# A streaming encoder step: keys of the running streams turned by VectorE's block transpose

## The chip, the cores and the metric

The kernel runs on one core of a Trainium2 chip. The metric is the device time of one execution in microseconds (us), as the median of several runs. TensorE (PE in the profile, with PEld for its weight loads) multiplies, VectorE (DVE), ScalarE (ACT) and GpSimd (POOL) work element by element, and SyncE (SP) issues every DMA of this kernel. Each engine runs its own queue of instructions in order and waits on semaphores for the others.

## The reference, cut to what matters

One inference step of a one-layer trunk. 1,024 rows of a new prompt and 8 running streams of 16 rows each, 1,152 rows of 1,024 columns, pass three token mixers (stick-breaking attention, Mamba-2, forgetting attention), then a cross-attention over 256 memory rows with 4 heads of 256 channels, and a SwiGLU. The running streams bring their own keys and values: 1,024 cached rows for each attention and 256 memory rows per stream. The change touches the places where their keys meet the queries:

```python
def sb_attend(q, k, v, q_pos, k_pos):            # k: past 1,024 rows and 16 new ones
    z = jnp.einsum('bqhd,bkhd->bhqk', q, k).astype(jnp.float32) * (HEAD_DIM ** -0.5)
    ...
def cross_attend(u, mk, mv, wq, wo):             # mk: cache_mem_k, (8, 256, 4, 256) for the streams
    q = jnp.einsum('bnd,de->bne', u, wq).reshape(b, n, X_HEADS, X_HEAD_DIM)
    s = jnp.einsum('bnhd,bmhd->bhnm', q, mk.astype(q.dtype)).astype(jnp.float32) * (X_HEAD_DIM ** -0.5)
    pr = jax.nn.softmax(s, axis=-1)
    o = jnp.einsum('bnhm,bmhd->bnhd', pr, mv.astype(jnp.float32)).astype(u.dtype)
    return jnp.einsum('bne,ed->bnd', o.reshape(b, n, D_MODEL), wo)
```

Both products sum over channels, so TensorE needs the keys with channels on the partitions, while memory holds them row by row.

## The kernel before, in words

Large products are made in three matmuls (`mm3`, lines 328 to 330): each factor is split into a rounded part `hi` (ACT, line 292) and a remainder `lo` (POOL in pieces of 256 columns, line 132), and hi x hi, hi x lo and lo x hi are summed in PSUM. Weights come in units of 1,024 columns (`w_unit`, line 307): two raw buffers of 528 columns, of which the ring has four (`wr`), are loaded (line 317) and split into a pair `wh`, `wl`, of which the ring has three each.

Stages in order of time: norm and memory projection; the stick-breaking attention with the input projection woven into it (about 140 to 430 us); the forgetting attention with Mamba-2 (to about 700); the output projection (`finish_rows`); the cross-attention (about 800 to 985), where each head's query projection (`x_query`) is woven with the attention of the head before (`x_prompt` for the prompt, `x_sample` for the streams); its output projection; the SwiGLU. The order of instructions on each engine is written by a scheduler that simulates the program with priorities, when the kernel is built; a change in one place can move instructions elsewhere.

The stick-breaking streams (`decode_units`, m = 0) work on two streams p at a time and half of the past (512 rows) at a time. `load_k` (lines 876 to 892) loads 512 rows of one stream in two DMAs into two raw buffers (line 882), PE turns eight blocks of 128x128 into two PSUM banks (line 888), and ACT copies them into `kf` (line 890), a buffer of the `wh` or `wl` ring. Four matmuls in four column groups (`quads`, line 873) then give 512 scores each. This happens 16 times; m = 1, the forgetting attention, has 16 more of the same code.

In `x_sample` two streams' memory rows of one head are loaded by two DMAs (line 1558), PE turns them in 8 transposes of 128x128 (line 1578), ACT copies one bank and DVE the other (line 1580) into `kf`, and `products` (line 1564) multiplies them with `zq`, the streams' queries placed so that each group of 32 PSUM rows gets two streams. There are 4 such loads a head. The channels of a head are split in two halves of 128, db, both for queries and keys.

## Time and profile before

| | us |
|---|---|
| Three runs, median (lowest to highest) | 1884.5 (1882.29 to 1886.88) |
| The profiled execution | 1882.33 |
| its span in the profile | 1880.6 |
| PE busy | 1826.0 |
| DVE busy | 886.7 |
| ACT busy | 802.5 |
| POOL busy | 618.4 |

In the profile's rows an instruction is named by its line in the kernel before, its engine and operation, and the tiles that it writes and reads ("pst<-ident,wr": into pst from ident and wr). A group's row gives the count, the time in which at least one of them ran, the mean of one in ns, and behind the next bar the engine's idle time just ahead of them and what ended it. A tile's row gives the shortest, middle and longest duration in ns and the first and last start. A row of the timeline gives start and duration. PE's matmuls overlap: one of 0.34 us may be followed by the next after 0.18.

### The profile page before, as it was taken

The page shows a single profiled execution, that of the slowest core. Times are in us where ns is not written, and L with a number is a line of the kernel's source. Part 1 is how long each engine was busy: PE and PEld are TensorE (multiplying, and loading weights), DVE is VectorE, ACT ScalarE, POOL GpSimd, SP SyncE. Part 2 cuts the span into 40 slices and gives each one's busy share as a digit, 9 for nine tenths or more (in the row PEclk, how much of TensorE's full clock was granted, in tenths as well). Part 3 has the DMA queues.
Part 4 walks back from the last instruction along what each step waited for, and adds up shares of the span by engine and source line. Part 5 has one row for each costly group of instructions (what it writes and reads, how often), then busy time and mean ns, then how long its engine had stood idle before and what let it go on. Part 6 is the DMA issues. An engine that isn't in the chain of part 4 may idle for free.

```text
span 1880.6 us, 32355 instructions
## 1 busy us (share of the span) xinstructions
PE 1826.0 (97%) x12136; PEld 1632.1 (87%) x12136; DVE 886.7 (47%) x1798; ACT 802.5 (43%) x1719; POOL 618.4 (33%) x921
## 2 busy tenths in 40 slices
PE   7999998999999999999999989999999999999998
PEld 5899877888967768899988889999999999888886
DVE  3412323475657862444443596333333334455554
ACT  6533543545456861344432464333333333344443
POOL 7622424445116663101112107445444542000000
PEclk9999999999999999999999999999999999999999
DMA  9465654437588882245585124333222223657572
GB/s 333 153 188 152 210 144 130 144 109 205 175 262 266 281 288 91 108 134 177 173 284 191 68 73 119 90 85 76 71 71 71 71 71 93 217 184 246 171 247 86
DMA packets 291036, 296.64 MB, mean 158 GB/s; under 512 B 80060, under 2 KB 242852, under 8 KB 290880
## 3 DMA queue, kind: packets, MB, share of 16 engines
q1 hardware_dynamic: 290880, 294.57, 49.9%
q8 instruction: 96, 1.57, 0.3%
q14 instruction: 60, 0.49, 0.1%
HBM read 225.12 MB, written 69.91 MB: 157 GB/s over the span
## 4 chain that ended last, share of the span: by engine, by line
PE 83%; DMA 5%; DVE 4%; POOL 3%; ACT 2%; issue 2%; SPq 0%; DVEq 0%; POOLq 0%; ACTq 0%
PE psd L1869 11%; PE psd L328 10%; PE psd L329 10%; PE psd L330 10%; PE pst L1869 8%; PE pss L1869 4%; PE pss L328 4%; PE pss L329 4%; PE pss L330 4%; PE pso L1869 2%; PE pst L328 2%; PE pst L329 2%; PE pst L330 2%; PE pso L593 1%; DMA act<-acsc 1%
## 5 line engine op out<-in xcount | busy, mean ns | idle before, releaser
L132 POOL TENSOR_TENSOR wl<-wr,wh 128x256 fp32r<-128x256 f32 (+2 forms) x184 | 142.3, 807 | 229.5 <-ACT wh L292 208.6
L328 PE MATMUL psd<-act,wh 128*128 128x384 f32 x528 | 182.3, 346 | 0.0
L330 PE MATMUL psd<-act,wl 128*128 128x384 f32 x528 | 181.2, 343 | 0.6 <-POOL wl L132 0.6
L329 PE MATMUL psd<-act,wh 128*128 128x384 f32 x528 | 181.7, 344 | 0.0
L1869 PE MATMUL pst<-bT,tr 128*128 128x256 f32 (+1 forms) x1068 | 155.0, 293 | 0.0
L1869 PEld LDWEIGHTS pst<-bT,tr 128*128 128x128 f32 x1068 | 144.9, 188 | 0.1
L330 PE MATMUL psd<-wh,act 128*128 128x512 f32 (+3 forms) x424 | 136.7, 323 | 0.0
L329 PE MATMUL psd<-wl,act 128*128 128x256 f32 (+3 forms) x414 | 134.0, 324 | 1.9 <-POOL wl L132 1.9
L328 PE MATMUL psd<-wh,act 128*128 128x256 f32 (+3 forms) x414 | 132.9, 325 | 0.7 <-DMA act<-osc 0.5
L1869 PE MATMUL psd<-bT,tr 128*128 128x320 f32 (+1 forms) x912 | 132.8, 295 | 0.6 <-POOL tr L132 0.6
L1869 PEld LDWEIGHTS psd<-bT,tr 128*128 128x128 f32 x912 | 124.7, 188 | 1.0 <-POOL tr L132 0.9
L132 POOL TENSOR_TENSOR tr<-u,tr 128x256 fp32r<-128x256 f32 x110 | 82.8, 781 | 101.7 <-ACT tr L1705 83.8
L253 POOL TENSOR_SCALAR sm<-sm 128x1 f32<-128x1 f32 (+2 forms) x27 | 9.1, 337 | 298.4 <-ACT y L1980 209.0
L1844 DVE TENSOR_TENSOR tr<-tr,pst 128x256 f32<-128x256 f32 (+1 forms) x86 | 38.6, 449 | 139.9 <-ACT tr L1841 106.6
L330 PEld LDWEIGHTS psd<-act,wl 128*128 128x128 f32 x528 | 99.2, 188 | 3.2 <-issue 1.9
L132 POOL TENSOR_TENSOR ws<-ws 128x256 f32<-128x256 f32 (+2 forms) x100 | 69.2, 719 | 98.7 <-DVE ws L522 90.4
L328 PEld LDWEIGHTS psd<-act,wh 128*128 128x128 f32 x528 | 99.4, 188 | 2.5 <-issue 1.8
L329 PEld LDWEIGHTS psd<-act,wh 128*128 128x128 f32 x528 | 99.3, 188 | 1.9 <-issue 1.5
L132 POOL TENSOR_TENSOR tr<-raw,tr 128x256 fp32r<-128x256 f32 x94 | 69.2, 764 | 83.8 <-ACT tr L1705 75.7
L1705 ACT CAST tr<-u 128x512 fp32r<-128x512 f32 x130 | 76.8, 620 | 28.6 <-PE pst L1869 5.6
L292 ACT CAST wh<-wr 128x512 fp32r<-128x512 f32 (+2 forms) x90 | 52.4, 621 | 82.9 <-PE psd L330 32.1
L329 PEld LDWEIGHTS psd<-wl,act 128*128 128x128 f32 x414 | 78.9, 191 | 10.0 <-POOL wl L132 3.6
(645 smaller groups left out, 4674.4 us busy)
## 6 DMA issues: line engine op xcount, KB each, us to landing
u<-w_down SPq DMA_DIRECT2D x40, 512.0 KB
raw<-w_down SPq DMA_DIRECT2D x26, 512.0 KB
st<-qksc SPq DMA_DIRECT2D x48, 256.0 KB
wr<-w_in SPq DMA_DIRECT2D x44, 256.0 KB
tr<-hidsc SPq DMA_DIRECT2D x55, 192.0 KB
hidsc<-tr SPq DMA_DIRECT2D x34, 288.0 KB
qksc<-sg SPq DMA_DIRECT2D x48, 192.0 KB
wr<-cache_sb_k SPq DMA_DIRECT2D x32, 256.0 KB
```

Of the source, the lines that this page charges most:

```text
L132: POOL.tensor_tensor(out=out[:, a0:a1], in0=in0[:, a0:a1], in1=in1[:, a0:a1], op=op)
L253: POOL.tensor_scalar(v, ss, inv, EPS, ALU.mult, ALU.add)
L292: ACT.copy(hi, raw)
L328: PE.matmul(out, ah, bh, start=start, stop=False)
L329: PE.matmul(out, ah, bl, start=False, stop=False)
L330: PE.matmul(out, al, bh, start=False, stop=stop)
L593: return PE.matmul(po[r:r + 64, q_], vt[:, 2 * (k0 + i) + j, :], pfs[i][:, sl], start=start and k0 == 0 and (j == 0 or qp > 0), stop=k0 + ...
L1705: ACT.copy(hi, src)
L1844: DVE.tensor_tensor(out=at(out, g), in0=at(x, g), in1=ps[g][:, :GW[g]], op=op)
L1869: PE.matmul(dst[g][:, :GW[g]], x[:, ka], y[:, k, :], start=start and k == 0 and m == 0, stop=stop and k == 3 and m == 2, skip_group_check= ...
```

## The change

**Memory keys of the streams.** Each load takes two streams' 512 rows of one head. Four DMAs bring it, one for each 64 channels into 32 partitions, 16 rows a partition in runs of 64 channels. DVE transposes blocks of 32x32 in place (`DVE.transpose`, STREAM_TRANSPOSE in the order). Then partition 32 g + j holds channels 64 g + 2 j and 64 g + 2 j + 1, so that the two halves of the channels are now the even and the odd ones. The keys are read by `products` in steps of two elements, and their rows come in another order (t, i), which the exponential of `x_softmax` puts back (`blocks`). The transposes on PE, the copies by ACT and DVE and the `kf` buffers go. Stream pairs are neighbours now (b0 + b for b0 + 2 b), which the placement of queries and the last transpose make good.

**Query weights.** The even and odd channels need `wq` split that way: `x_query` makes two units of 256 columns by four row blocks, both needed by each half db, with a split that sorts columns by parity (`split_parted`: ACT and POOL read in steps of two; as many instructions as before). The prompt's memory keys are turned on PE from every second column (`mkn[:, mb, db::2]`).

**Cached stick-breaking keys.** `load_k` for m = 0 loads one stream's 512 rows in four DMAs into one raw buffer, runs of 32 channels (128 bytes), and DVE transposes 128x1024 from it into `kf`, writing in steps of 16 elements. Eight transposes on PE and two copies by ACT go. m = 1 stays as it was.

**Raw buffers.** The ring has two of 1,056 columns where it had four of 528; `w_unit` and `load_k` use the two halves of one.

The core of the diff:

```diff
--- before.py
+++ after.py
@@ -302,12 +302,23 @@
 
     def raw_t():
 
-        return ring.tile([P, 528], F32, tag="wr", name="wr", bufs=4)
-
-    def w_unit(srcs, k0, nk, raw=None, pair=None, eng=POOL):
+        return ring.tile([P, 1056], F32, tag="wr", name="wr", bufs=2)
+
+    def split_parted(hi, lo, raw):
+        h, l = (t.rearrange("p (k x m) -> p k x m", x=2, m=P) for t in (hi, lo))
+        r = raw.rearrange("p (k m x) -> p k x m", x=2, m=P)
+        ACT.copy(h, r)
+        for k in range(h.shape[1]):
+            POOL.tensor_tensor(out=l[:, k], in0=r[:, k], in1=f32(h[:, k]), op=ALU.subtract)
+
+    def w_unit(srcs, k0, nk, raw=None, pair=None, eng=POOL, parted=False):
 
         n = sum(s[2] for s in srcs)
-        raws = [raw_t(), raw_t()] if raw is None else [raw]
+        if raw is None:
+            raw = raw_t()
+            raws = [raw[:, :528], raw[:, 528:]]
+        else:
+            raws = [raw]
         nk_ = nk // len(raws)
         for i, r in enumerate(raws):
             rv = r[:, :nk_ * n].rearrange("p (k n) -> p k n", n=n)
@@ -320,7 +331,10 @@
         hi, lo = pair or unit_pair()
         for i, r in enumerate(raws):
             sl = slice(i * nk_ * n, (i + 1) * nk_ * n)
-            split_into(hi[:, sl], lo[:, sl], r[:, :nk_ * n], eng)
+            if parted:
+                split_parted(hi[:, sl], lo[:, sl], r[:, :nk_ * n])
+            else:
+                split_into(hi[:, sl], lo[:, sl], r[:, :nk_ * n], eng)
         return (hi[:, :nk * n].rearrange("p (k n) -> p k n", n=n),
                 lo[:, :nk * n].rearrange("p (k n) -> p k n", n=n))
 
@@ -874,9 +888,17 @@
                                                 moving(g // 2, g % 2), start=True, stop=True) for g in (3, 0, 1, 2)])
 
             def load_k(hf, b2):
-                rvs = []
+                if m == 0:
+                    raw = raw_t()[:, :1024]
+                    src = ck[2 * p + b2, hf * 512:(hf + 1) * 512, :].rearrange("(i t) (n g j) -> g i (t n) j", t=16, n=2, g=4)
+                    for g in range(4):
+                        SP.dma_start(out=raw[32 * g:32 * g + 32].rearrange("i (b j) -> i b j", j=32), in_=src[g])
+                    kf = ring.tile([P, 1056], F32, tag=("wh", "wl")[b2], name="kf")
+                    DVE.transpose(kf[:, :1024].rearrange("c (n i t) -> c t n i", n=2, t=16), raw)
+                    return kf
+                rvs, rt = [], raw_t()
                 for q in range(2):
-                    rvs.append(raw_t()[:, :512].rearrange("p (k c) -> p k c", c=256))
+                    rvs.append(rt[:, 528 * q:528 * q + 512].rearrange("p (k c) -> p k c", c=256))
                     k0 = hf * 512 + q * 256
 
                     SP.dma_start(out=rvs[q], in_=ck[2 * p + b2, k0:k0 + 256, :].rearrange("(p k) c -> p k c", k=2))
@@ -1449,16 +1471,29 @@
                 DVE.scalar_tensor_tensor(lo, src, XQS, f32(hi), ALU.mult, ALU.subtract)
                 if c == 2:
                     ACT.activation(qs[:, db, :], ps[:, 256:384], AF.Copy, scale=XQS)
-            return ((2 * hd + db) * P, consume)
+            return db, consume
+        units = [w_unit([(wq, 256 * hd, 256)], k0, 4, parted=True) for k0 in (0, 4)]
         for db in range(2):
-            yield from dense_T(wq, uc, [job(db)])
-
-    def x_softmax(ps, n, pr):
+            _, consume = job(db)
+            for c in range(NCH):
+                ps = pd()
+                uh, ul = uc[c]
+                for k in range(KT):
+                    wh, wl = (t[:, k % 4, db * P:(db + 1) * P] for t in units[k // 4])
+                    mm3(ps[:, :CW], wh, wl, uh[:, k, :], ul[:, k, :], k == 0, k == KT - 1)
+                consume(c, ps[:, :CW])
+                flush()
+                yield
+
+    def x_softmax(ps, n, pr, blocks=None):
         mx, su = small(2 * n), small(2 * n)
         DVE.tensor_reduce(out=mx[:, 0:n], in_=ps, op=ALU.max, axis=AX)
         DVE.tensor_scalar(mx[:, n:2 * n], mx[:, 0:n], -1.0, None, ALU.mult)
         for i in range(n):
-            ACT.activation(pr[:, i * 256:(i + 1) * 256], ps[:, i, :], AF.Exp, bias=mx[:, n + i:n + i + 1],
+            to, of = pr[:, i * 256:(i + 1) * 256], ps[:, i, :]
+            if blocks:
+                to, of = to.rearrange("q (i t) -> q t i", t=blocks), of.rearrange("q (t i) -> q t i", t=blocks)
+            ACT.activation(to, of, AF.Exp, bias=mx[:, n + i:n + i + 1],
                            accum_out=su[:, i:i + 1])
         DVE.reciprocal(su[:, n:2 * n], su[:, 0:n])
         for i in range(n):
@@ -1477,7 +1512,7 @@
         tp = pT()
         for db in range(2):
             for mb in range(2):
-                PE.transpose(tp[:, db * 256 + mb * P:db * 256 + (mb + 1) * P], mkn[:, mb, db * P:(db + 1) * P], ident)
+                PE.transpose(tp[:, db * 256 + mb * P:db * 256 + (mb + 1) * P], mkn[:, mb, db::2], ident)
         tv = tp.rearrange("p (d m) -> p d m", d=2)
         ACT.copy(kt[:, 0], tv)
         DVE.tensor_tensor(out=kt[:, 1], in0=tv, in1=f32(kt[:, 0]), op=ALU.subtract)
@@ -1548,41 +1583,45 @@
     def x_sample(hd, q):
         qs = q[2]
         for db in range(2):
-            POOL.tensor_copy(*put_streams(db, qs[:, db, :]))
+            dst, _ = put_streams(db, qs[:, db, :])
+            POOL.tensor_copy(dst, qs[:, db, :].rearrange("p (e i t) -> p i e t", e=2, t=DEC_S))
 
         def mem_rows(src, b0):
 
             raw = ws_t()
             rv = raw[:, :1024].rearrange("p (b m c) -> p b m c", b=2, m=2)
             for b in range(2):
-                SP.dma_start(out=rv[:, b], in_=src[(b0 + 2 * b) * 256:(b0 + 2 * b + 1) * 256, hd * 256:(hd + 1) * 256]
+                SP.dma_start(out=rv[:, b], in_=src[(b0 + b) * 256:(b0 + b + 1) * 256, hd * 256:(hd + 1) * 256]
                              .rearrange("(m p) c -> p m c", p=P))
             return rv
 
         def products(ps, e, moving):
 
-            together([lambda i=i, x=x, b=2 * i + e: PE.matmul(
-                ps[32 * i:32 * i + 32, :256], zq[:, x, 32 * b:32 * b + 32], moving(i, x),
+            def out(i, m):
+                o = ps[32 * i:32 * i + 32, :256]
+                return o if len(m.shape) == 2 else o.rearrange("p (t i) -> p t i", i=DEC_S)
+
+            together([lambda i=i, x=x, b=2 * i + e, m=moving(i, x): PE.matmul(
+                out(i, m), zq[:, x, 32 * b:32 * b + 32], m,
                 start=e == 0 and x == 1, stop=e == 1 and x == 0) for x in (1, 0) for i in (3, 0, 1, 2)])
 
         ps = pS()
         for e in range(2):
             kfs = []
             for i0 in (0, 2):
-                rv = mem_rows(cmk, 2 * i0 + e)
-                kf = ring.tile([P, 1056], F32, tag=("wh", "wl")[i0 // 2], name="kf")
-                for b in range(2):
-                    tp = pT()
-                    for db in range(2):
-                        for mb in range(2):
-                            PE.transpose(tp[:, db * 256 + mb * P:db * 256 + (mb + 1) * P],
-                                         rv[:, b, mb, db * P:(db + 1) * P], ident)
-                    (DVE.tensor_copy if b else ACT.copy)(kf[:, b * 512:(b + 1) * 512], tp)
-                kfs.append(kf)
+                raw = ws_t()[:, :1024]
+                k0 = (4 * e + i0) * 256
+                for g in range(4):
+                    SP.dma_start(out=raw[32 * g:32 * g + 32].rearrange("i (t c) -> i t c", c=64),
+                                 in_=cmk[k0:k0 + 512, hd * 256 + 64 * g:hd * 256 + 64 * g + 64]
+                                 .rearrange("(i t) c -> i t c", t=16))
+                blocks = raw.rearrange("p (t j x) -> p t x j", x=2, j=32)
+                DVE.transpose(blocks, blocks)
+                kfs.append(raw.rearrange("p (t i x) -> p x t i", x=2, i=32))
                 if i0:
-                    products(ps, e, lambda i, x: kfs[i // 2][:, i % 2 * 512 + x * 256:i % 2 * 512 + (x + 1) * 256])
+                    products(ps, e, lambda i, x: kfs[i // 2][:, x, :, i % 2 * 16:i % 2 * 16 + 16])
                 yield
-        pr = x_softmax(ps[:, :256].rearrange("p (i m) -> p i m", i=1), 1, sg_t())
+        pr = x_softmax(ps[:, :256].rearrange("p (i m) -> p i m", i=1), 1, sg_t(), 16)
         tp = pT()
         for mb in range(2):
             PE.transpose(tp[:, mb * P:(mb + 1) * P], pr[:, mb * P:(mb + 1) * P], ident)
@@ -1591,7 +1630,7 @@
         yield
         po = pS()
         for e in range(2):
-            rvs = [mem_rows(cmv, e), mem_rows(cmv, 4 + e)]
+            rvs = [mem_rows(cmv, 4 * e), mem_rows(cmv, 4 * e + 2)]
             yield
             products(po, e, lambda i, x: rvs[i // 2][:, i % 2, x, :])
             yield
@@ -1599,7 +1638,8 @@
         ACT.copy(on[:, :256], po[:, :256])
         tp = pT()
         for db in range(2):
-            PE.transpose(tp[:, db * P:(db + 1) * P], on[:, db * P:(db + 1) * P], ident)
+            PE.transpose(tp[:, db * P:(db + 1) * P].rearrange("p (e i t) -> p i e t", e=2, t=DEC_S),
+                         on[:, db * P:(db + 1) * P], ident)
         x_out(hd, (tp[:, 0:P], tp[:, P:2 * P]), SEQ, P)
         yield
```

**In the order of instructions.** PE's order has 11,034 matmuls, before 11,290; DVE's has 32 more transposes and 16 fewer copies; ACT's 48 fewer copies; SP's 64 more DMAs. Lines of the change are numbered by its own file there. PE, the first stick-breaking keys of the streams (L888 transposes keys, L873 multiplies them; in the change L887 multiplies them; L328 to L330 and L342 to L344 are the input projection), before:

```order
L329 MATMUL psd<-act,wh 128x384
L888 MATMUL pst<-ident,wr 128x128 x4
L330 MATMUL psd<-act,wl 128x384
L888 MATMUL pst<-ident,wr 128x128 x8
L873 MATMUL pss<-kf,st 32x512 x4
L888 MATMUL pst<-ident,wr 128x128 x8
L471 MATMUL pst<-ident,pt 128x128 x3
L578 MATMUL pst<-ident,ws 128x128 x8
```

and in the change:

```order
L342 MATMUL psd<-act,wh 128x384
L343 MATMUL psd<-act,wh 128x384
L344 MATMUL psd<-act,wl 128x384
L887 MATMUL pss<-kf,st 32x512 x8
L342 MATMUL psd<-act,wh 128x384
```

The transposes between the projection's matmuls are gone, and the two halves' products (4 and 4) stand together. DVE, the same place in the change (L897 transposes keys; L470 and L467 take the projection out of PSUM, L536 scans a row of the prompt's attention, L487 copies transposed prompt keys); before, DVE had no part in the keys:

```order
L470 SCALAR_TENSOR_TENSOR sg<-psd,sg 128x384
L536 SCALAR_TENSOR_TENSOR ws<-ws 128x384
L897 STREAM_TRANSPOSE kf<-wr 128x16x64 x2
L470 SCALAR_TENSOR_TENSOR sg<-psd,sg 128x384
L536 SCALAR_TENSOR_TENSOR ws<-ws 128x512
L470 SCALAR_TENSOR_TENSOR sg<-psd,sg 128x384
L536 SCALAR_TENSOR_TENSOR ws<-ws 128x640
L470 SCALAR_TENSOR_TENSOR sg<-psd,sg 128x384
L897 STREAM_TRANSPOSE kf<-wr 128x16x64 x2
```

Pairs of transposes now stand in DVE's queue between evictions of the psd banks. DVE, the start of the cross-attention in the change (L279 finishes the norm's transposed rows, L1471 takes queries out of PSUM, L1619 transposes memory keys):

```order
L279 SCALAR_TENSOR_TENSOR act<-pst,cols,act 128x384
L1619 STREAM_TRANSPOSE ws<-ws 128x16x2x32
L279 SCALAR_TENSOR_TENSOR act<-pst,cols,act 128x384 x2
L1619 STREAM_TRANSPOSE ws<-ws 128x16x2x32
L279 SCALAR_TENSOR_TENSOR act<-pst,cols,act 128x384
L1619 STREAM_TRANSPOSE ws<-ws 128x16x2x32
L279 SCALAR_TENSOR_TENSOR act<-pst,cols,act 128x384
L1471 SCALAR_TENSOR_TENSOR st<-psd,st 128x384
```

Before, copies (L1580) stood some rows later, behind the norm; three of the first four transposes now stand between its last rows.

## The prediction

> **What bounds the kernel now.** I read the page's totals first, then the chain of work that ended last, then the busy times of the two stages that the change touches.
>
> ```profile
> PE 1826.0 (97%) x12136; PEld 1632.1 (87%) x12136; DVE 886.7 (47%) x1798; ACT 802.5 (43%) x1719; POOL 618.4 (33%) x921
> PE 83%; DMA 5%; DVE 4%; POOL 3%; ACT 2%; issue 2%; SPq 0%; DVEq 0%; POOLq 0%; ACTq 0%
> ...
> 140.00:430.00 290.00, 276.21 (x2042) 246.60 (x2040) 114.93 (x195) 125.84 (x292) 111.57 (x178) 0.99 0.50 147
> 430.00:700.00 270.00, 257.97 (x2086) 208.89 (x2085) 181.90 (x481) 162.87 (x365) 131.90 (x210) 0.99 0.79 250
> 800.00:985.00 185.00, 184.48 (x1371) 172.03 (x1370) 86.09 (x201) 72.83 (x195) 22.15 (x37) 1.00 0.57 189
> ```
>
> The columns of the last three rows are the stretch in us, its length, then busy time of PE, PEld, DVE, ACT and POOL, the granted clock, the busy share of the DMA engines and GB/s. TensorE bounds both stages: 14 us idle of 290 in the stretch that holds the cached stick-breaking keys, half a microsecond of 185 in the cross-attention. DVE, ACT and POOL are each under half busy there and the DMA engines stand at 0.50 and 0.57. So what leaves PE is worth its whole time, as long as the four others deliver no later than now.
>
> **What is removed.** The program's order has 11,034 matmuls now and had 11,290: 256 transposes go, 128 of cached stick-breaking keys (line 888, half of its 256) and 128 of memory keys (line 1578). Their busy time must not be taken as it stands, since neighbours overlap:
>
> ```profile
> L888 PE MATMUL pst<-ident,wr 128*128 128x128 f32 x256 | 38.2, 278 | 3.9 <-DMA wr<-cache_sb_k 2.7 <-ACT kf L890 0.8 <-DMA wr<-cache_fox_k 0.3
> L1578 PE MATMUL pst<-ident,ws 128*128 128x128 f32 x128 | 20.7, 273 | 0.0
> ...
> 193.75 0.34 PE L328 MATMUL psd<-act,wh 128*128 128x384 f32 x1
> 193.92 0.34 PE L329 MATMUL psd<-act,wh 128*128 128x384 f32 x1
> 194.10 0.60 PE L888 MATMUL pst<-ident,wr 128*128 128x128 f32 x4
> 194.45 0.42 PE L330 MATMUL psd<-act,wl 128*128 128x384 f32 x1
> 194.71 0.33 PE L328 MATMUL psd<-act,wh 128*128 128x384 f32 x1
> ...
> 831.06 0.44 PE pst L1578 x4
> 838.68 1.00 PE pss L1564 x16
> ```
>
> A 128x384 matmul starts 0.175 us after the one before. From 193.92 to 194.71 are 0.79 us with two of them, so four transposes cost 0.79 - 0.35 = 0.44 us; the chain books the same 0.44 us for four memory-key transposes. That is 0.11 us each: 256 x 0.11 = **-28.2 us**. Upper bound by the groups' busy time: 38.2 / 2 + 20.7 = 39.8 us. Lower bound: only the cross-attention's half, 14.1 us, if something other than PE takes over in the first stage.
>
> ACT and DVE lose the copies out of PSUM, 32 of the 64 of line 890 and all 32 of line 1580, 0.59 to 0.69 us each:
>
> ```profile
> L890 ACT COPY kf<-pst x64: 566/588/660, 192.5 to 664.0; 128x512 f32<-128x512 f32 x64
> L1580 ACT COPY kf<-pst x16: 583/586/609, 818.6 to 974.3; 128x512 f32<-128x512 f32 x16
> L1580 DVE COPY kf<-pst x16: 668/692/692, 819.2 to 974.8; 128x512 f32<-128x512 f32 x16
> ```
>
> ACT is off the path, so I count nothing for its 28 us.
>
> **What is added on DVE.** 32 block transposes of 128x1024. No such operation is in the trace; its nearest rows are passes over 1,024 columns:
>
> ```profile
> L771 DVE SCALAR_TENSOR_TENSOR xc<-xc,cols 128x1024 f32<-128x1024 f32 x24 | 32.0, 1333 | 0.0
> L522 DVE TENSOR_TENSOR_SCAN ws<-ws 128x1024 f32<-128x1024 f32 x4 | 9.5, 2376 | 4.5 <-ACT ws L519 4.5
> L271 DVE TENSOR_SCALAR ws<-st,sm 128x1024 f32<-128x1024 f32 x8 | 5.6, 750 | 0.2
> ```
>
> Between 0.75 and 2.4 us; I take 1.3 us, the ordinary pass. In the first stage that is 16 x 1.3 = 21 us (38 at most) on top of 115 in 290; in the cross-attention 21 - 11 = 10 us net (27 at most) on top of 86 in 185. DVE stays below two thirds either way, so the work lies beside PE's. What it can cost is a late result: before its keys have landed a transpose holds the DVE queue, and behind it wait evictions of the psd banks and the scan. A psd bank takes 24 matmuls of 0.175 us, 4.2 us, and there are two, so PE does not feel a DVE hold of up to about 4 us. Now the hand-over of keys makes PE wait 3.9 us before line 888. I add **+2 us** for the new one (0 to 8, twice the present).
>
> **What moves.** The key loads come in short runs, 128 bytes for stick-breaking (1,024 runs in each of four DMAs, where there were two DMAs of 2 KB runs), 256 bytes for memory keys (from 1 KB).
>
> ```profile
> DMA packets 291036, 296.64 MB, mean 158 GB/s; under 512 B 80060, under 2 KB 242852, under 8 KB 290880
> 150.54 0.37 SPq L510 DMA_DIRECT2D st<-vsc  x1
> 151.60:153.00 1.40, 1.40 (x10) 1.40 (x9) 0.00 (x0) 0.53 (x2) 1.40 (x4) 1.00 1.03 236
> ...
> L882 SPq DMA_DIRECT2D wr<-cache_sb_k x32: 328/346/541, 153.0 to 420.9; - x32
> L510 SPq DMA_DIRECT2D st<-vsc x8: 370/402/1203, 150.5 to 619.2; - x8
> L1558 SPq DMA_DIRECT2D ws<-cache_mem_k x32: 367/440/470, 804.3 to 955.2; - x32
> ...
> 267.42 2.34 DMA wr<-cache_sb_k
> ```
>
> The value load of line 510 moves 256-byte runs, and the stretch behind it shows all engines busy at 236 GB/s: 16 x 256 / 236 = 17.4 ns a packet. The stage from 430 to 700 us, of mixed sizes, gives 250 / 0.79 = 316 GB/s. So a 128-byte packet costs at most 17.4 ns and at least half: one key load of 4,096 packets takes 2.2 to 4.5 us where 512 KB at 316 GB/s took 1.7. All 16 add 8 to 45 us to 145 us (0.50 x 290) of DMA time; the memory keys 512 KB / 236 - 512 KB / 316 = 0.6 us a load, 9 us beside 105. Both fit. SP issues 64 DMAs more at 0.35 to 0.44 us, and line 510 shows that 1,024 runs do not lengthen an issue. Weights and query stacks behind them on SP's queue start 0.7 us later for a load's two more issues; that is covered as far as they are fetched a unit ahead.
>
> Two reads become strided by 8 bytes: the moving keys of line 1564 (128 matmuls, 1.00 us for 16) and 16 transposes of prompt keys. The trace has one such read, the weight load of line 924 in steps of 16 bytes:
>
> ```profile
> L888 PEld LDWEIGHTS pst<-ident,wr x256: 137/140/230, 190.5 to 659.6; 128*128 128x128 f32 x128
> L924 PEld LDWEIGHTS pst<-ident,ws x72: 137/210/222, 221.2 to 685.7; 128*128 128x128 f32 x72
> ```
>
> Half as long again. Bounds for 8-byte steps are nothing and that: 8 x 1.00 x 0.5 = 4 us, and 16 x 0.07 = 1 us. I take half, **+2.5 us**. [...]
>
> **Raw buffers and the query weights.** Two buffers of 1,056 columns hold what four of 528 held, but come free only when both halves are split. And each head's first query matmuls need both weight units, where one was enough. At the end of the output projection the second unit's buffer is given up 18 matmuls of 0.23 us and then 12 of 0.175 us before it is needed, 6.3 us; to fill it takes two casts and four subtractions, 2 x 0.62 + 4 x 0.74 = 4.2 us, the first half of them 2.1:
>
> ```profile
> 793.28 0.23 PE psd L328
> L292 ACT CAST wh<-wr x90: 602/620/662, 63.3 to 1042.0; 128x512 fp32r<-128x512 f32 x82, 128x520 fp32r<-128x520 f32 x4, 128x528 fp32r<-128x528 f32 x4
> L132 POOL TENSOR_TENSOR wl<-wr,wh x184: 196/740/2972, 68.1 to 1043.4; 128x256 fp32r<-128x256 f32 x176, 128x8 fp32r<-128x8 f32 x4, 128x16 fp32r<-128x16 f32 x4
> ```
>
> SP already stands before a key load until its buffer is free, and what is queued behind it stands too:
>
> ```profile
> SPq L882 <- PE pst L888: 28.7, 14, 10.3
> ```
>
> Then it waits for DVE instead of PE. I count nothing; 4 us once if ACT is busy with the norm's squares just then. On the credit side the memory keys no longer take turns with weights in the wh and wl buffers.
>
> **Sum.** -28.2 + 2 + 2.5 = -23.7 us. The profiled execution took 1882.3 us (span 1880.6 and 1.7 around it), the median of the runs is 1884.5, 2.2 above: 1882.3 - 23.7 = 1858.6, and on the median's footing about **1860 us**, 1.3% faster.
>
> **Rivals.** (1) *The first stage gives its half back.* For it: PE idles 14 us there, and waits on key loads, weights and POOL, so its neighbours are near; raw buffers freed in pairs hold the weights longer. Against: DMA at half, POOL at 112 of 290 us. Only the cross-attention's 14.1 us less 4.5 stay: 1884.5 - 9.6 = 1875 us.
>
> (2) *Slower: DVE stands before keys that come in short runs.* One stream pair's four loads pass through two raw buffers; each must land (4.5 us of packets and the 2.3 us that the chain shows for such a load, 6.8 us) before DVE turns it, and all evictions stand behind. It decides from the point where the hold outlasts the psd banks' 4.2 us. If 8 of the 16 loads are that late and wholly uncovered, 54 us come on: 1884.5 - 23.7 + 54.4 = 1915 us. Against it: SP issues the first key loads at 153 us and PE turned them at 190. [...]
>
> (3) *More than the sum:* each transpose also broke up the stream, and 39.8 us go: 1884.5 - 39.8 + 2 = 1847 us.
>
> (4) *It doesn't do what it says* would need the transposes still to be there; the order shows them gone, so it gets no chance.
>
> **How the numbers follow.** Forecast (1851 to 1868) 0.55; rival 1 (1868 to 1880) 0.22; rival 3 (1843 to 1851) 0.08; gain and late keys cancel 0.05; rival 2 or a smaller form of it 0.10. The range 1846 to 1880 holds the first two and most of the third, 0.8 in all. A measurement tells 0.2%, 3.8 us, from no change: faster 0.55 + 0.22 + 0.08 = 0.85, same 0.05, slower 0.10.
>
> **What would show it.** In the profile after: no PE rows of memory-key transposes and 128 of line 888's kind, PE's busy time some 26 us lower, its idle time near the present 55 us; block transposes of about 1.3 us; the key products still near 1.00 us for 16; DVE's waits on the key loads a few us in all. I am wrong if PE's idle time grows by more than 10 us, with waits of PE on DVE behind a transpose, or of DVE on a key load, at the top.

## The result: 0.9% slower, and the profile after

The changed kernel takes 1901.1 us as the median of four runs (1900.14 to 1905.68), beside 1884.45 for the kernel before: 1.0092 times as long, 95% interval 1.0079 to 1.0105. The profiled execution of the changed kernel is the slowest of its four, 1905.7 us with a span of 1904.0; the other three lie 4 to 5.5 us lower, which is to be kept in mind where its parts are read.

The page of the changed kernel, busy times and DMA packets:

```profile
PE 1819.5 (96%) x11880; PEld 1620.2 (85%) x11880; DVE 931.5 (49%) x1814; ACT 778.4 (41%) x1671; POOL 614.9 (32%) x921
DMA packets 373977, 296.59 MB, mean 156 GB/s; under 512 B 179388, under 2 KB 329892, under 8 KB 373824
```

The 256 transposes are gone, but PE is busy only 6.5 us less, not 28. Its idle time grew from 54.6 to 84.5 us. So some 22 us of what was taken away came back as longer matmuls, and 30 us as waits. The same stretches as in the prediction, then two shorter ones, in the changed kernel, and behind them the two shorter ones in the kernel before. Columns: the stretch, its length, busy PE, PEld, DVE, ACT, POOL, granted clock, DMA share, GB/s.

```profile
140.00:430.00 290.00, 265.91 (x1914) 234.56 (x1913) 145.11 (x204) 111.95 (x264) 113.28 (x178) 0.95 0.61 148
430.00:700.00 270.00, 258.11 (x1994) 209.39 (x1996) 185.22 (x483) 156.49 (x352) 121.31 (x199) 0.96 0.74 238
800.00:985.00 185.00, 179.81 (x1258) 166.76 (x1256) 90.37 (x191) 69.01 (x181) 32.03 (x51) 0.98 0.69 180
280.00:300.00 20.00, 11.73 (x51) 8.97 (x50) 14.73 (x38) 5.98 (x14) 11.85 (x23) 0.50 0.34 38
965.00:1025.00 60.00, 43.44 (x249) 34.12 (x249) 20.17 (x51) 11.82 (x38) 2.22 (x5) 0.83 0.86 275
```

```profile
280.00:300.00 20.00, 16.00 (x140) 14.11 (x140) 10.28 (x14) 8.27 (x19) 16.59 (x25) 0.91 0.61 164
965.00:1025.00 60.00, 59.48 (x381) 49.57 (x380) 28.68 (x64) 21.70 (x58) 17.21 (x25) 1.00 0.82 288
```

Two places stand out. From 280 to 300 us PE works 12 of 20 us, all of it at half clock. From 965 to 1025 us, where PE had been full, it lacks 16 us and the clock falls to 0.83. What PE waits for longest (us in total, times, longest; the first row is the program's start, 6.7 us in the kernel before), and the groups of the new and the changed instructions, in the changed kernel:

```profile
PE pst L219 <- DMA xc<-conv_w: 7.0, 1, 7.0
PE pss L342 <- ACT pt L1496: 6.6, 2, 5.4
PE psd L696 <- POOL st L883: 6.4, 1, 6.4
PE psd L344 <- DMA act<-osc: 3.6, 2, 1.9
PE pst L946 <- POOL ws L132: 3.4, 2, 3.1
PE pss L1604 <- DVE ws L1619: 3.1, 1, 3.1
...
L897 DVE STREAM_TRANSPOSE kf<-wr 128x1024 f32<-128x1024 f32 x16 | 30.9, 1961 | 27.4 <-DMA wr<-cache_sb_k 9.4 <-issue 6.9 <-PE pss L887 5.7
L1619 DVE STREAM_TRANSPOSE ws<-ws 128x1024 f32<-128x1024 f32 x16 | 19.9, 1245 | 21.6 <-DMA ws<-cache_mem_k 20.3 <-issue 1.2
L1604 PE MATMUL pss<-ws 128*32 128x256 f32 x256 | 16.4, 388 | 3.1 <-DVE ws L1619 3.1
```

The block transposes lie within the bounds of the prediction, and the key products did not slow down. Of the five waits behind the program's start only the last is for a transpose. Two others stand next to each other about 280 us: line 946 turns the attention weights of a pair of streams in the stick-breaking attention and waits for a multiplication on POOL, and line 696 is the first product of the forgetting attention's sums. (The row puts that wait down to a copy on POOL that ended at 289.0 us; the product's own operand, `lf`, was finished by DVE at 288.9.) The last two are in the last head of the cross-attention (an exponential, and the stacks of `osc`).

### The profile page after: what moved, and what is told of

It is laid out like the page before. It is cut to its first block, busy times and chain, and to the rows that moved or that the text cites. A ratio compares the mean times of both kernels' runs of the same rounds, so it can differ in the third digit from the quotient of the medians.

```text
span 1904.0 us, 31811 instructions
## 1 busy us (share of the span) xinstructions
PE 1819.5 (96%) x11880; PEld 1620.2 (85%) x11880; DVE 931.5 (49%) x1814; ACT 778.4 (41%) x1671; POOL 614.9 (32%) x921
## 5 line engine op out<-in xcount | busy, mean ns | idle before, releaser
L132 POOL TENSOR_TENSOR wl<-wr,wh 128x256 fp32r<-128x256 f32 (+2 forms) x152 | 114.7, 787 | 253.9 <-ACT wh L292 253.0
L342 PE MATMUL psd<-act,wh 128*128 128x384 f32 x528 | 182.5, 346 | 0.8 <-DVE sg L470 0.8
L344 PE MATMUL psd<-act,wl 128*128 128x384 f32 x528 | 179.9, 341 | 0.0
L344 PE MATMUL psd<-wh,act 128*128 128x512 f32 (+3 forms) x424 | 139.1, 330 | 3.6 <-DMA act<-osc 3.6
L342 PE MATMUL psd<-wh,act 128*128 128x256 f32 (+3 forms) x414 | 135.6, 331 | 5.4 <-DMA act<-osc 2.2
L342 PEld LDWEIGHTS psd<-act,wh 128*128 128x128 f32 x528 | 99.4, 188 | 4.9 <-issue 1.9
L344 PEld LDWEIGHTS psd<-act,wl 128*128 128x128 f32 x528 | 99.2, 188 | 1.0 <-issue 0.8
L342 PEld LDWEIGHTS psd<-wh,act 128*128 128x128 f32 x414 | 80.7, 195 | 15.5 <-DVE lf L506 3.6
L344 PEld LDWEIGHTS psd<-wh,act 128*128 128x128 f32 x424 | 82.2, 194 | 11.6 <-DMA act<-osc 4.5
```

Source lines behind the costliest of these rows:

```text
L132: POOL.tensor_tensor(out=out[:, a0:a1], in0=in0[:, a0:a1], in1=in1[:, a0:a1], op=op)
L342: PE.matmul(out, ah, bh, start=start, stop=False)
L344: PE.matmul(out, al, bh, start=False, stop=stop)
```

## Where the time went: a ledger in three stretches

Two rows split the program well: the evictions of the query projection (line 1449 before, 1471 after) and the additions of the output projections (1322, 1344), which ran first before the cross-attention and last behind it. First the kernel before, then the changed one; the two times ahead of the semicolon are the first and last start.

```profile
L1322 DVE TENSOR_TENSOR st<-st,psd x16: 677/686/689, 701.6 to 1035.7; 128x512 f32<-128x512 f32 x16
L1449 DVE SCALAR_TENSOR_TENSOR st<-psd,st x24: 411/554/558, 803.7 to 968.6; 128x384 fp32r<-128x384 f32 x16, 128x256 fp32r<-128x256 f32 x8
L1322 DVE TENSOR_TENSOR xc<-xc,psd x4: 686/688/689, 718.6 to 1041.3; 128x512 f32<-128x512 f32 x4
```

```profile
L1344 DVE TENSOR_TENSOR st<-st,psd x16: 675/686/689, 711.1 to 1057.5; 128x512 f32<-128x512 f32 x16
L1471 DVE SCALAR_TENSOR_TENSOR st<-psd,st x24: 387/542/559, 813.9 to 964.7; 128x384 fp32r<-128x384 f32 x16, 128x256 fp32r<-128x256 f32 x8
L1344 DVE TENSOR_TENSOR xc<-xc,psd x4: 680/686/689, 727.4 to 1063.1; 128x512 f32<-128x512 f32 x4
```

The attention stages end (first addition) 9.5 us later, where I wanted 14 earlier. The query stretch, first to last eviction, shrank from 164.9 to 150.8 us. That this is the 14.1 us of the forecast to the decimal is luck: only three of the four heads' transposes, 10.6 us, stood in it, and the rest is work that now comes behind the last query. And the tail, from the last query eviction to the last addition, grew from 72.7 to 98.4 us, which took them back and 11.6 more. All that follows the tail lasts 839 to 841 us in every run of this study, and from the first addition to the first query eviction it is 101 to 104, so both are left out below. The same three readings for each kernel's profiled execution, with the median of all its runs:

| kernel | median us | ratio to before, 95% | attention ends | query stretch | tail | query + tail |
|---|---|---|---|---|---|---|
| before | 1884.5 | | 701.6 | 164.9 | 72.7 | 237.6 |
| changed | 1901.1 | 1.0092 (1.0079 to 1.0105) | 711.1 | 150.8 | 98.4 | 249.2 |
| e1 raw buffers alone | 1892.6 | 1.0038 (1.0025 to 1.0051) | 709.0 | 165.2 | 72.4 | 237.6 |
| e2 e1 + stick-breaking keys | 1888.2 | 1.0015 (1.0001 to 1.0030) | 701.9 | 164.8 | 72.3 | 237.1 |
| e3 e1 + memory keys | 1902.5 | 1.0091 (1.0064 to 1.0119) | 708.3 | 150.6 | 97.9 | 248.5 |
| e4 e2, long runs | 1885.0 | 0.9997 (0.9980 to 1.0014) | 702.6 | 165.0 | 72.9 | 237.9 |
| e5 e3, long runs | 1901.7 | 1.0085 (1.0065 to 1.0105) | 710.4 | 159.7 | 88.5 | 248.2 |
| e6 e3, last head on PE | 1892.3 | 1.0039 (1.0024 to 1.0054) | 709.7 | 151.8 | 86.1 | 237.9 |
| e7 e2, sums woven | 1891.7 | 1.0034 (1.0023 to 1.0046) | 707.4 | 165.0 | 72.5 | 237.5 |
| e8 e1, sums woven | 1899.3 | 1.0075 (1.0051 to 1.0099) | 718.6 | 165.2 | 72.6 | 237.8 |
| e9 e3, keys in the ring | 1893.2 | 1.0039 (1.0019 to 1.0059) | 705.5 | 152.6 | 86.2 | 238.8 |
| e10 before, SB transposes twice | 1900.7 | 1.0071 (1.0049 to 1.0094) | 719.9 | 165.1 | 72.7 | 237.8 |
| e11 before, memory transposes twice | 1899.6 | 1.0074 (1.0049 to 1.0098) | 701.2 | 177.2 | 76.4 | 253.6 |
| e12 SB keys, old raw buffers | 1883.7 | 0.9984 (0.9966 to 1.0002) | 701.9 | 165.6 | 73.2 | 238.8 |
| e13 e12, waits filled | 1906.2 | 1.0122 (1.0100 to 1.0145) | 718.5 | 165.4 | 72.6 | 238.0 |
| e15 e9, old raw buffers | 1885.3 | 1.0009 (0.9995 to 1.0022) | 702.4 | 152.8 | 85.0 | 237.8 |
| e16 e15 with e13 | 1906.5 | 1.0117 (1.0096 to 1.0139) | 718.3 | 152.9 | 86.2 | 239.1 |
| e17 e15, writes first | 1881.9 | 1.0000 (0.9986 to 1.0015) | 703.0 | 152.9 | 82.6 | 235.5 |
| e18 e17 + SB keys | 1880.9 | 0.9979 (0.9968 to 0.9989) | 701.6 | 152.7 | 82.3 | 235.0 |

(SB: the cached stick-breaking keys. The stretches are those of one profiled execution; where medians and stretches differ by some us, the median weighs more. The kernel before was run again beside each group of experiments, with medians from 1884.2 to 1886.3 us. Each ratio is to those runs and taken over all runs, so it is not the quotient of two medians of the table.)

## The experiments

### The three parts apart (e1, e2, e3)

e1: the kernel before with `raw_t` of 1,056 columns, two of them. e2: e1 with the new branch of `load_k`. e3: the changed kernel with that branch taken out.

> Only the two raw buffers of 1,056 columns for four of 528; every transpose stays on PE and every load as before. If the raw buffers cause the loss (theory R), this alone is 10 to 25 us slower than before, 1895 to 1910 us. If the loss lies in the key loads (theory L: short packets hold the DMA engines and SP's queue) or in the order of the first stage (theory O: the chain of the forgetting attention's sums stands with no product beside it), it is within 6 us of before, 1879 to 1891 us.

> Raw buffers and cached stick-breaking keys as changed, cross-attention as before. The changed kernel reaches the cross-attention 9.5 us later than before, so if the stages add up (O and L alike) this gives about 1894 us (1889 to 1900) with the granted clock at half for some 24 us about 280 us. By my forecast's mechanism alone it would be 1884.5 - 14 = 1870 us.

> Raw buffers, query weights and memory keys as changed, cached stick-breaking keys as before (PE transposes, long runs). From the start of the output projection's first eviction to the first product of the SwiGLU the changed kernel takes 420.3 us where before takes 407.8, so L and a late tail give 1884.5 + 12 = 1897 us (1890 to 1902); theory O, by which the loss hangs on the first stage alone, gives 1870 to 1884 us.

The raw buffers, which I had at nothing, cost 0.38%, 7 us; "within 6 us" was just missed. The stick-breaking part gives back 4 us of that, not 14. The memory part costs 10 us more: the whole +11 in its query stretch and tail, as in the changed kernel. In e2 and in the changed kernel the instructions of every engine stand in the same order to the end of the attention stages, so the 9 us by which the two profiled executions differ there come from the execution, not from the order: the granted clock of the changed kernel's execution was at half for 17 us at 562 us, where that of e2 was full (1.00 from 560 to 700 us). One profile's reading of these stages is thus uncertain by as much as 9 us. Of the 16.6 us between the medians of the changed kernel and of the one before, query stretch and tail account for 11.6, so these stages for some 5.

### Are the short runs the cause? (e4, e5)

```diff
-  four DMAs a load, 128-byte (e4) or 256-byte (e5) runs, 32 partitions each
+  two DMAs a load, 2 KB (e4) or 1 KB (e5) runs, 128 partitions each, as before
```

> As the run with only the stick-breaking keys changed, but each load is two DMAs of 2 KB runs as before, so the block transposes work on rows in the wrong place and the scores of the cached keys are not the reference's: only the time is read. Theory L: the loss of that part goes, 1868 to 1878 us, and the half clock about 280 us with it. Theory O: within 5 us of the run with short runs, about 1894 us, since the order on PE is nearly the same.

> As the run with only the memory keys changed, but each load is two DMAs of 1 KB runs as before in place of four of 256-byte runs; the block transposes then work on rows in the wrong place, so the streams' cross-attention scores are not the reference's and only the time is read. Theory L (the short packets fill the DMA engines and SP's queue, so the last head's keys, the stacks of line 1404 behind them and the writes into osc come late): most of the 9.9 us between that run (1902.5) and the one with the raw buffers alone (1892.6) goes, and part of the 14 us that were to be gained shows, 1880 to 1893 us, with PE's idle time between 940 and 1060 us below 6 us. Theory O (PE lacks cover in the last head once its transposes are gone): 1898 to 1904 us.

Not for the most part. e4 gains 3 us on e2, with intervals that overlap; e5 gains nothing on e3, though its loads come in runs of 1 KB as before. In e5 only the share changes: the query stretch is longer and the tail shorter, the sum is 248 us again. The rate is low, though. A stretch of the changed kernel in which the memory keys' loads fill the DMA engines:

```profile
947.00:953.00 6.00, 6.00 (x40) 6.00 (x39) 1.00 (x3) 1.96 (x7) 0.00 (x0) 1.00 1.13 189
```

189 GB/s at a share of 1.13, in packets of 311 bytes in the mean (3,634 of them, 1.13 MB), where the same engines moved 370 at 1.07 from 965 to 1000 us of the kernel before, in packets of 1.3 KB (9,952, 12.96 MB), and where the prediction took 236 from the value loads. Theory L falls: at most the 3 us of e4 hang on the short runs of the stick-breaking keys, and nothing that e5 could show on those of the memory keys.

### The first stage (e7, e8, e12, e13, e16)

In e2 as in the changed kernel PE stands in the forgetting attention's sums, a chain of some twenty small DVE steps (lines 419 to 427, 672 and 692 to 694 there) between the last input projection and the next one. First the chain's beginning, its middle and its end on DVE in the kernel before. Then, from e12, where only the stick-breaking keys are changed and the raw buffers are the old four, DVE and PE:

```profile
267.30 0.38 DVE L406 RECIPROCAL sg<-sg 128x36 f32<-128x36 f32 x1
...
271.52 0.20 DVE L658 SCALAR_TENSOR_TENSOR lf<-lf,sg 128x36 f32<-128x36 f32 x1
...
271.95 1.15 DVE L680 TENSOR_TENSOR so<-so,lf 128x4 f32<-128x4 f32 x6
```

```profile
268.36 0.38 DVE L406 RECIPROCAL sg<-sg 128x36 f32<-128x36 f32 x1
...
274.25 2.50 DVE L522 TENSOR_TENSOR_SCAN ws<-ws 128x896 f32<-128x896 f32 x1
276.67 1.62 DVE L411 SCALAR_TENSOR_TENSOR sg<-sg 128x36 f32<-128x36 f32 x3
278.33 0.65 DVE L412 SCALAR_TENSOR_TENSOR sg<-sg 128x36 f32<-128x36 f32 x1
279.01 0.18 DVE L413 TENSOR_SCALAR sg<-sg 128x36 f32<-128x36 f32 x1
279.23 0.52 DVE L658 SCALAR_TENSOR_TENSOR lf<-lf,sg 128x36 f32<-128x36 f32 x1
...
285.43 0.71 DVE L680 TENSOR_TENSOR so<-so,lf 128x4 f32<-128x4 f32 x2
```

```profile
275.57 0.41 PE L563 MATMUL pss<-mask_sb,identr 128*128 128x128 f32 x1
279.80 0.64 PE L682 MATMUL psd<-lf,sg 128*128 128x32 f32 x2 [3.82 <-DVE lf L658]
...
293.40 0.42 PE L328 MATMUL psd<-wh,act 128*128 128x264 f32 x1
...
299.92 0.28 PE L328 MATMUL psd<-wh,act 128*128 128x264 f32 x1
```

A scan of 2.5 us stands among the small steps, PE waits 3.8 us for the last of them, and the products behind it take 0.42 us each where the same ones take 0.28 from 298 us on: the clock is at half from 274 to 298 us. Before, the transposes of the next keys and their hand-over stood in this place.

The chain itself has also become longer. From its reciprocal to its last addition it took 5.8 us before and takes 17.8 in e12. Five scans of the stick-breaking attention (line 522), 8.4 us of them, now stand among its steps; before, the first of these scans came at 279.8 us, behind it. In the new order the attention runs further ahead (the products of a prompt's row of 896 columns come at 267.6 us, before 279.8), and its scans with it. The same holds for all profiles. In the twelve kernels in which PE turns the stick-breaking keys the chain takes 5.5 to 6.1 us, with no such scan in it. In seven of the eight in which DVE turns them it takes 16 to 19 us, with 5 to 8.5 us of scans (the eighth is e7 below). So DVE did deliver later, though not for a transpose in the chain. No run had the keys on DVE and these scans behind the chain in an order otherwise as in e12.

e12's edit and result:

```diff
+  raws = [raw_t()[:, :512] for _ in range(2)]      # two of the four old buffers
+  ... eight DMAs, two DVE.transpose of 128x512 into kf
```

> Stick-breaking keys by block transposes, but with the four raw buffers of 528 columns: one load is eight DMAs of half the rows each into two buffers and two block transposes of 128x512. Cross-attention as before. If the raw buffers' 8.2 us and the keys' -4.4 us add up: 1880 us (1876 to 1884), a little faster than before. If the gain only showed because the raw buffers had slowed the stage down: 1884 to 1888.

With nothing else changed, 128 transposes fewer end the attention stages at 701.9 us, before 701.6, and the ratio leaves a gain of 3 us, by its interval at most 6, of the 14.1. PE's busy time is 1820.0 us, 6.0 less, and its idle time 61.5, 6.9 more: of 14.1 us taken away 8.1 came back as longer matmuls (the mean granted clock was 0.987, some 49 us of the span at half; before it was 0.994, some 23) and 6.9 as waits. That the transposes had covered the chain, and that the chain grew, are two readings of the same rows; the runs do not part them. The raw buffers cost something where PE turns the keys: six profiles end the attention stages between 705 and 712 us (e1, e3, e5, e6, e9, e14), beside 702 to 703 for the four old ones (e15, e17). Which wait that is was not settled. Whether they cost as much beside the new keys can't be told: by the ratios, e1's +0.38% and e12's -0.16% add up to e2's +0.15% within the intervals, and the profiles say 701.9 us (e2) and 711.1 (the changed kernel) for the same order.

Two attempts to put cover back:

```diff
 e7, e8:  zs = z_proj(0);  for _ in fox_sums(): next(zs); yield
 e13:     PE.transpose(tp, ident, ident)   # 28 and 24 times, behind a step of the sums
```

> As the run with raw buffers and stick-breaking keys changed, but the first z projection is woven into the forgetting attention's sums, four of its blocks between their steps, where the PE waits of 3 and 6 us stood. Theory O (the transposes had covered that chain; without them PE waits and its granted clock is halved for some 25 us): 1888.2 goes to 1872 to 1881 us, half-clock time falls below 30 us. Theory L: within 3 us of 1888.

> The control for the covered run: raw buffers alone as changed, all transposes on PE, and the same weaving of the z projection. Theory O: with the transposes in place there is little to cover, 1885 to 1893 us beside 1892.6 without weaving. If it gains as much as the run with the keys changed, the weaving is a gain by itself and says nothing on the transposes.

> As the run with stick-breaking keys by block transposes and the four old raw buffers (1883.7 us), plus 54 transposes of the identity on PE that nothing reads, 5.9 us at 0.11, placed where PE waits 3.8 and 3.3 us for DVE in the forgetting attention's sums. If the waits halve the granted clock (theory K), the half-clock stretch of 23.9 us at 285 us goes and with it some 10 us: 1872 to 1879 us, though PE has more to do. If the clock does not follow the waits: 1884 to 1890.

> Stick-breaking keys by block transposes with old raw buffers, the identity transposes in the waits, and the memory keys in wh and wl buffers. If e13 and e15 each bring what theories K and S say, some 10 and 8 us off 1884: 1862 to 1872 us, faster than both kernels. By theory C alone: 1880 to 1886.

All four came out slower (e7 by 3.5 us, its interval just meeting e2's). Weaving costs 7 us in the control e8 and 3.5 in e7, so the keys' worth beside it is 7.6 us instead of 4.4. In e7 the chain takes 9.0 us and holds none of these scans, but PE still waits 2.4 and 5.4 us in it: a hint, not more, and for theory O and a longer chain alike. With the identity transposes the clock is higher from 280 to 300 us, 0.86 for 0.55 in e12 (0.66 for 0.71 from 270 to 280):

```profile
280.00:300.00 20.00, 16.25 (x82) 14.43 (x83) 10.49 (x24) 4.88 (x11) 12.61 (x22) 0.55 0.27 44
```

```profile
280.00:300.00 20.00, 16.43 (x114) 14.07 (x115) 12.53 (x21) 9.36 (x21) 12.41 (x24) 0.86 0.48 70
560.00:700.00 140.00, 124.09 (x985) 94.44 (x985) 99.44 (x288) 91.85 (x206) 81.62 (x132) 0.98 0.80 261
```

(the first row e12, the other two e13). But the chain still takes 16.8 us in e13, the order of everything behind it changed, and between 560 and 700 us PE lost 16 of 140 us, in e12 8. So the clock was higher in this one place with part of the waits filled, 0.86 for 0.55; that this would win the 14 us was not shown.

### What a transpose costs (e10, e11)

```diff
-  PE.transpose(tp[...], rv[...], ident)
+  for _ in range(2): PE.transpose(tp[...], rv[...], ident)
```

> The kernel before with each of the 128 PE transposes of cached stick-breaking keys done twice. At the full price of 0.11 us each, as my forecast took it, 14.1 us more: 1898.6. If the first stage is held by chains of DVE, ACT and POOL beside which the transposes run (theory C), 2 to 6 us more: 1887 to 1891.

> The kernel before with each of the 128 PE transposes of memory keys done twice. Full price: 1898.6 us. Theory C for the cross-attention (three heads pay, and what they pay comes off the tail again): the stretch from the first to the last query eviction grows by about 10 us from 166.9, the one from there to the first product of the SwiGLU shrinks from 125.9, and the time is 1886 to 1892 us.

e11 is clear: the span grew by 15.1 us, 0.118 us for each of 128, 12.3 of it in the query stretch and 3.7 in the tail. (By the ratio of all runs it is 13.9 us or 0.109 each, with an interval from 9 to 18 us.) The tail did not give it back, as I had expected of theory C: work added to PE costs its price there, though work removed is not won. e10 took 14 us more as well, 18 by the profile's first stages. It can't be read as a price: e8 and e13, which only reorder or add 6 us of work, moved the end of these stages by 10 and 17 us.

### The cross-attention's tail (e6, e9, e14, e15, e17)

What SP issues around the last head, first in the kernel before, then in the changed one (start, duration, line, tiles, count):

```profile
952.76 1.40 SPq L1558 DMA_DIRECT2D ws<-cache_mem_k  x3
...
964.43 2.10 SPq L1504 DMA_DIRECT2D osc<-pt  x4
968.13 10.45 SPq L1382 DMA_DIRECT2D act<-osc  x8
```

```profile
962.55 0.98 SPq L1404 DMA_DIRECT2D act<-osc  x2
...
968.34 8.45 SPq L1615 DMA_DIRECT2D ws<-cache_mem_k  x5
...
983.74 4.77 SPq L1404 DMA_DIRECT2D act<-osc  x4
...
997.78 2.61 SPq L1539 DMA_DIRECT2D osc<-pt  x4
...
ACT pt L1496 <- DMA osc<-pt: 18.1, 1, 18.1
```

Before, the last head's keys were issued by 956 us, then the third head's last outputs were written, then the stacks for the output projection loaded. After, keys are still issued at 968 us, one DMA taking up to 2.3 us to issue, with the DMA engines at a share of 1.07 from 968 to 977 us, and the writes come at 998 us, behind everything. The last row is ACT's longest wait there (4.4 us for such a write before): an exponential needs a `pt` buffer that such a write still holds. PE's wait of 5.4 us for line 1496 hangs on it. The transposed keys stay in `ws` until `products` has read them, and `ws` has six buffers beside `zq`; before, they moved on into `kf`.

```diff
 e6:  heads 0 to 2 as changed, head 3 as before
 e9:  kf = ring.tile([P, 1056], F32, tag=("wh", "wl")[i0 // 2]);  DVE.transpose(kf.., raw..)
 e15: e9 with raw_t of 528 columns, four of them
 e17: e15, and DVE.tensor_copy(first[c][:, x, 0, 0:2], seen) ahead of load_chunk,
      where seen is taken from the third head's last outputs
```

> As the run with only the memory keys changed, but the fourth head's memory keys, query weights and placement are as before (1 KB runs, PE transposes); heads 0 to 2 as changed. All that stalls PE in the cross-attention lies in the last head, so both theories expect most of the 9.9 us back and some of the three heads' 10.6 us of transposes gained: 1882 to 1893 us. If it stays at 1898 or more, the loss comes from the first three heads' loads.

> As the run with only the memory keys changed, but DVE transposes each load out of its ws buffer into a wh or wl buffer, as the keys lay before, so that the ws buffer is free after the transpose and not after the products. Theory B (the keys hold six ws buffers, so the last head's keys and values are loaded only in the tail, where DMA is full, and SP's queue is held): the last key loads are issued before 965 us again and the time is 1884 to 1893. Theory C (with the query products done 15 us earlier the tail lacks work on PE whatever the buffers): 1898 to 1904 us as before this edit.

> A look at the run with the memory keys in the wh and wl buffers again, beside the next one: 1889 to 1898 us.

> Memory keys by block transposes out of ws into wh and wl buffers (1893.2 with two raw buffers of 1,056), but with the four raw buffers of 528 as before; stick-breaking keys as before. If the raw buffers cost the first stages 8 us and nothing else: 1885. If SP's waits for them also hold the writes of osc in the tail (theory S): 1870 to 1880, and PE's wait of 7.7 us for the exponential of line 1488's kind goes. If the tail lacks work on PE whatever the buffers (theory C): 1883 to 1887 with that wait still there.

> As e15, but before a stack of line 1392's kind is loaded, DVE writes two of its columns from a value of the third head's last output, so that the six large loads stand behind the last writes into osc in SP's queue. If the order of writes and loads causes the tail's wait (theory D): PE's wait of 6.1 us for the exponential goes, the tail shrinks from 138 to 126 to 131 us, 1872 to 1879 us, faster than before. If DMA is simply full there (theory L): the loads now come late for the output projection instead, 1883 to 1892.

Theory B holds for its part: with the keys in the ring (e9; e14 is the same kernel again) the last key load is issued at 947.6 us, the query stretch and tail go from 248.5 to 238.8 us and the time falls by 9 us. Four raw buffers (e15) bring the first stages back and leave the tail as it is, so theory S falls. In e15 SP's order still had the loads ahead of the writes; e17 turned that round, and 2 us came of it, with intervals that overlap. Rows of e15, then of e17:

```profile
956.68 10.76 SPq L1392 DMA_DIRECT2D act<-osc  x8
976.45 4.30 SPq L1527 DMA_DIRECT2D osc<-pt  x4
...
PE pss L338 <- ACT pt L1484: 7.3, 2, 6.1
```

```profile
966.48 2.60 SPq L1530 DMA_DIRECT2D osc<-pt  x4
969.17 7.28 SPq L1392 DMA_DIRECT2D act<-osc  x6
...
PE pss L338 <- ACT pt L1484: 6.0, 1, 6.0
...
955.00:985.00 30.00, 21.17 (x139) 17.56 (x138) 12.13 (x41) 11.78 (x34) 9.21 (x13) 0.83 1.00 343
```

The writes come 10 us earlier and PE still waits 6 us: the first product of the output projection now starts at 975.8 us, where it started at 966.8 in e15, and no longer stands ahead of that wait. The DMA engines are full for all of these 30 us. They were so before, too:

```profile
955.00:1000.00 45.00, 44.48 (x321) 38.76 (x320) 20.39 (x48) 17.70 (x50) 8.81 (x13) 1.00 1.05 359
```

There PE had work for 44.5 of the 45 us in which the engines were full. e6 says the same from another side: with three heads changed and the fourth as before, 96 transposes of 0.11 us are gone, the query stretch is 13 us shorter, and the tail is 13 us longer, some 3 of them work that moved behind the last query. Beside e1, which has the same raw buffers, e6 gains nothing (1892.3 and 1892.6 us). I read the tail as a chain of values, writes, loads and output products at full DMA, with the queries of the last head as its cover, so that removing work ahead of it lengthens it. That is argued from these rows: no run removed the rest of it, about 10 us, and loading the stacks before the queries are done, which needs their buffers earlier, was not tried.

### Both keys, with what was learned (e18)

e18 is e17 with e12's `load_k`.

> As e17, with the stick-breaking keys by block transposes out of the four raw buffers too (1883.7 us alone, 0.7 to 2.6 us below before). Theory D and adding up: 1870 to 1878 us. If the first stage's order falls worse again, as in the run with identity transposes, 1885 or more.

1880.9 us, 0.9979 of before (0.9968 to 0.9989): the one version that is faster than both kernels, by 0.2% where the forecast had 1.3, and short of the 1870 to 1878 us that I expected of it. PE is busy 1807.5 us there, 18.5 less than before, and idle 70.3. The loss against the kernel before is so accounted for, by the four raw buffers (1.0039 in e9, 1.0009 in e15) and the keys' place (1.0091 in e3, 1.0039 in e9). What stays open is why 28 us less on PE are worth only 4: the first stage's chain and the tail are where they went, and no run brought them back.

## Why the prediction was wrong, step by step

- **The step that failed** is the sentence from the totals: "what leaves PE is worth its whole time, as long as the four others deliver no later". Taken alone, the first stage's 14.1 us were worth 3 (e12, at most 6) and the memory keys' 14.1 us nothing, even with their buffers put right (e15, 1.0009). The condition failed too: DVE, at half its time busy, finished the sums' chain in 17.8 us where it had taken 5.8, because other work moved into it. A PE at 97% was read as a PE that bounds everywhere, and an engine at 50% as one that can't be late. What would have shown it is the place of each transpose: what stands beside it, what PE has left there without it, and what the new order puts between the steps of the chains nearby.
- **The price, -28.2 us at 0.11**, was right as what a transpose adds: 0.118 by e11's profile, 0.109 by its ratio. As what its removal wins it was not: PE's busy time fell by 6.5 us.
- **"Its idle time near the present 55 us"** was the sign I named, with 10 us more as the sign of error. It grew by 30. The waits that were to stand at the top with it did not: PE waited for a transpose once, 3.1 us.
- **Block transposes at 1.3 us (0.75 to 2.4)**: 1.25 in place, 1.96 with the output in steps of 16 elements. Rightly bounded, and off the path by the 3.1 us that PE waited for them; the chain that DVE finished late was another.
- **Strided reads, +2.5 us**: nothing. 379 ns median a key product before and after.
- **Key loads**: that more runs "do not lengthen an issue" was wrong: 0.63 us median (up to 2.3) for line 1615 and 0.67 (up to 2.7) for 895, where I took 0.35 to 0.44. It had no effect that e4 and e5 could show beyond their intervals.
- **Raw buffers, counted at nothing**: +7 us alone (e1).
- **The keys' buffers**: "the memory keys no longer take turns with weights in the wh and wl buffers" stood on the credit side. It was the largest single loss, 10 us (e9): they took the place of the next loads in `ws` instead.
- **The rivals**: the first, that the first stage gives its half back, came true for that half, but with DVE (the chain of 17.8 us) and the clock (0.55 from 280 to 300 us in e12), not with the key loads, weights and POOL that it named. The slower one had the sign and the wrong mechanism: DVE did stand for late keys, 9.4 and 20.3 us, but long runs won nothing clear of their intervals (e4, e5). The loss came by ways that I hadn't listed: the keys' buffers, the raw buffers, and a tail at full DMA. The forecast, 1860 us, the range to 1880 and the 0.85 on faster all missed.

## What to carry to other kernels

A busy share of 97% says that PE bounds on the average, not at each place: before work is counted as won, look at what runs beside it and whether a chain of other engines or a full DMA would then be in the open, and in the new order, what now stands between that chain's steps; adding the same work (e11) and removing it are not opposites. When an operand is no longer copied on, ask which ring now holds it until its last use, and what is queued for that ring. And where a scheduler orders the program, compare stretches rather than totals, for a few instructions more or less moved the end of other stages by 10 us and more; and profile more than once, for two executions of the same order of these stages ended 9 us apart.

## What the runs showed of the hardware

In the traces of the two kernels the granted clock is recorded at full or at half. In the profile of the changed kernel the half stretches last 3.41, 6.83, 17.07 and 23.89 us, and 5.7 us at the end of the program, 84 us in all where before had 23. Two half stretches stand at waits of PE. In the changed kernel the clock fell at 279 us, 1 us behind a wait of 3.2 us, stayed so through one of 6.4 us, and was full again at 303 us, 14 us behind the second. In e12 it fell at 274.3 us with the end of a wait of 2.3 us, and stayed at half to 298 us, though PE was busy for 11.4 of the 12 us from 286 us on; what ends a half stretch these rows do not show. So in these two places the half clock lasted some 24 us, beside waits of PE of 9.6 us in all in the one and 9.4 in the other (2.3, 3.8 and 3.3).
